# Pinning the cast and split of the re-read tokens to their place in the source

## The chip, the cores and the metric

The kernel runs on one core of one Trainium2 chip. The metric is the device time of one execution in microseconds (us); the median of several executions is compared. Lower is better.

The core has engines that run side by side and each take their own instructions in order: TensorE (PE in the profile; its weight loads are PEld), VectorE (DVE), ScalarE (ACT), GpSimd (POOL) and SyncE (SP), which here only starts DMA transfers. An instruction that must wait for another engine or for a transfer holds up everything behind it on its own engine.

## The reference, cut to what matters

One step of a hybrid decoder layer with 256 prompt tokens and 8 samples of 8 tokens each: a mixer (a pooling branch and a state-space branch, "SSD", with 64 heads in 8 groups), a cross-attention and a gated MLP. The change sits in the state-space branch, where the recurrent state of the 8 samples is brought up to date:

```python
def step(h, inp):
    s, d = inp
    return h * d[..., None, None] + s, h
...
chunk_states = jnp.einsum('bcsgn,bcsgr,bcsgrp->bcgrpn', bm, to_end, xd)
```

For every group and sample, the new state is the old one times a decay, plus a product over the sample's 8 tokens of their B row (128 numbers) and their weighted x row (512 numbers).

## The kernel before

All dense products work in three matmuls on fp32r operands: a weight tile of 128x1024 ("unit", `raw`) is loaded, cast to `wh` on ScalarE (L82), and its remainder `wl` is taken on VectorE (L83); then TensorE runs L88 (wh by the high part of the activations), L89 (wh by the low part) and L90 (wl by the high part). The buffers of `raw` are 4 deep, those of `wh` and `wl` 3, the accumulators `acc` 4 and the other PSUM tiles `misc` 4. One matmul of 320 columns follows the last after 0.15 us.

`mixer_ssd` goes through 8 groups. In each it writes out a list of dense jobs, and after a job the small steps of the state-space branch that `ssd` lists by job number. From the second to the seventh group the jobs are: 0 to 5 the six xBC columns of the next group, 6 to 13 the eight jobs `ssm_out` of the group before (24 matmuls each; their two sums are added into `accs` by VectorE at L711, in the second group copied by ScalarE at L709), then four gate jobs. In the first group jobs 6 to 9 are `gate_pool` columns of 48 matmuls, in the last one jobs 0 to 5 are.

The steps that matter here, with the job after which they are written:

- 4: `states`, whose result `fin` is stored, and `off_sample`
- 5: `diagonal` (matmuls L594, VectorE's sum L596 out of PSUM), and `rows_in(0)`, `rows_in(1)`: the sample tokens that were stored to DRAM are read again, each sample's 8 rows four times, into `rw` (two tiles of 128x640, L558)
- 6: `off_prompt` (matmuls L605, VectorE L606) and `off_sample_out` for both halves (transposes L201 into `misc`, VectorE L628); after job 7, `add_off` (GpSimd, L655)
- 8 and 10: `rows_split(0)`, `rows_split(1)`: ScalarE casts `rw` to `rh` (L565), VectorE takes from `rw` a part of `rh` that depends on the row (L568, once for 512 columns, once for 128)
- 9 and 12: `update(0)`, `update(1)`: four matmuls each (L644) on the split rows; VectorE adds them to the decayed state `hin` (L648)
- 9 and 11 of the next group's list: `decays` (VectorE L488, 24 small scalings of tables `g` and `gs_` that a DMA has brought, then exponentials on ScalarE, L490)

`rh`, `fin` and one more tile share one buffer (tag `fin`), so each cast L565 also waits until that buffer's last reader is done: the store of `fin`, or L568 of the half before. The xBC jobs end in three taps on VectorE (L443) between ScalarE's L441 and L447.

The program is not run in the order of writing. A scheduler reorders it at build time: it puts an instruction into its engine's queue when it believes its operands ready, by priority, and units are given a head start of 300 places. `keep_in_program_order(ins)` adds an edge for the order alone, without a wait: `ins` stands behind the instruction of its engine that was written last before it.

Of the kernel before, what the change touches and what calls it, by code (L numbers as in the profile page):

```python
# [11 lines left out]
F32 = mybir.dt.float32  # L12
F32R = mybir.dt.float32r
AF = mybir.ActivationFunctionType
ALU = mybir.AluOpType
# [42 lines left out]
class Kernel:  # L58
# [397 lines left out]
    def ssd(self, s, g):  # L456

        nc, I, O = self.nc, self.I, self.O
# [102 lines left out]
        def rows_split(q):  # L561

            rw = v["rw", q]
            rh = s.tile([128, 640], F32R, tag="fin", name="rh")
            nc.scalar.copy(out=rh, in_=rw)  # L565
            rr = v["rr"] = rw.bitcast(F32R)
            for c, w_ in ((C_RX, slice(0, 512)), (C_RB, slice(512, 640))):
                nc.vector.scalar_tensor_tensor(out=rr[:, w_], in0=rh[:, w_].bitcast(F32), scalar=self.cst[:, c:c + 1],  # L568
                                               in1=rw[:, w_], op0=ALU.mult, op1=ALU.add)

        def states():
            bt, xw = v["bt"], v["xw"]
# [81 lines left out]
        def add_off():  # L654
# [13 lines left out]
            6: [off_prompt, lambda: off_sample_out(0), lambda: off_sample_out(1)],  # L668
            7: [add_off],
            8: [lambda: rows_split(0)],  # L670
            9: [lambda: update(0)],
            10: [lambda: rows_split(1)],
            11: [lambda: store_states(0)],
            12: [lambda: update(1)],
# [595 lines left out]
```

## Time and profile before

| what | value |
|---|---|
| median of 3 executions | 2934.41 us (2933.08 to 2935.30) |
| profiled execution, its own time | 2932.04 us |
| its span | 2930.2 us |
| PE (matmul) busy | 2903.8 us, 99% |
| PEld busy | 2821.0 us, 96% |
| DVE busy | 1768.9 us, 60% |
| ACT busy | 1304.7 us, 45% |
| POOL busy | 454.4 us, 16% |
| granted TensorE clock, mean | 0.998 |

The profile shows one execution. Busy time is the time in which an engine had an instruction under way; matmul ends are modelled, so starts are the surer reading. A view by waits names the waiting instruction, the one that released it, the total in us, the number of times and the longest. A timeline row gives start and duration in us, engine, source line, operation, the tile written and those read, the shape, how many instructions are merged (x) and, in brackets, how long the engine had been idle before and who ended that.

### The profile page before, as it was taken

What the parts mean: (1) busy time and instruction counts of PE and PEld (TensorE: products, weight loads), DVE (VectorE), ACT (ScalarE), POOL (GpSimd) and SP (SyncE); (2) the same over time, 40 slices, a digit from 0 to 9 for tenths busy, and PEclk for the clock granted to TensorE, in tenths of its full rate; (3) what the DMA queues carried; (4) which work ended last, traced back from release to release, by engine and by line L of the source; (5) the groups of instructions that cost most, each with busy time, mean ns of one, the idle gap of its engine ahead of it and who ended that gap; (6) DMA issues with size and microseconds to landing.
All of it is one profiled execution on the core that took longest, in us unless ns stands there. A gap on an engine that the chain in (4) does not pass through costs nothing.

```text
span 2930.2 us, 50017 instructions
## 1 busy us (share of the span) xinstructions
PE 2903.8 (99%) x20105; PEld 2821.0 (96%) x20105; DVE 1768.9 (60%) x2662; ACT 1304.7 (45%) x1866; POOL 454.4 (16%) x567
## 2 busy tenths in 40 slices
PE   9999999999999999999999999999999999999998
PEld 7999999999999999999999999999999999999997
DVE  5667576686776755554355555567666646645644
ACT  6535565455454444344333443345444434433434
POOL 3113132142231220231111100011000000000002
PEclk9999999999999999999999999999999999999999
DMA  7775655655645645544445477754444444444443
GB/s 280 245 229 190 228 188 171 222 159 197 225 154 202 225 151 186 181 154 164 152 171 187 151 252 281 262 184 154 151 154 149 155 151 151 151 153 148 153 151 115
DMA packets 173385, 536.93 MB, mean 183 GB/s; under 512 B 21344, under 2 KB 48224, under 8 KB 168928
## 3 DMA queue, kind: packets, MB, share of 16 engines
q1 hardware_dynamic: 162272, 515.14, 52.1%
q10 hardware_dynamic: 10880, 18.58, 1.8%
q8 instruction: 158, 2.59, 0.4%
q14 instruction: 75, 0.61, 0.1%
HBM read 497.09 MB, written 36.56 MB: 182 GB/s over the span
## 4 chain that ended last, share of the span: by engine, by line
PE 84%; DVE 8%; issue 2%; ACT 2%; DMA 2%; POOL 2%; SPq 0%; POOLq 0%; ACTq 0%; DVEq 0%
PE acc L88 27%; PE acc L89 26%; PE acc L90 26%; DVE wl L83 3%; DVE ca L443 1%; POOL hin L637 1%; ACT wh L82 1%; DVE g L488 1%; DMA raw<-in_w_ssm_out_dram 1%; DVE accs L711 1%; PE misc L981 1%; PE misc L943 1%; PE acc L239 0%; PE acc L240 0%; PE acc L238 0%
## 5 line engine op out<-in xcount | busy, mean ns | idle before, releaser
L83 DVE TENSOR_TENSOR wl<-raw,wh 128x1024 fp32r<-128x1024 f32 (+1 forms) x795 | 986.9, 1242 | 808.7 <-ACT wh L82 807.1
L82 ACT CAST wh<-raw 128x1024 fp32r<-128x1024 f32 (+1 forms) x795 | 829.9, 1045 | 1207.1 <-PE acc L89 830.4
L88 PE MATMUL acc<-a0h,wh 128*128 128x320 f32 (+1 forms) x2704 | 837.2, 310 | 0.0
L90 PE MATMUL acc<-a0h,wl 128*128 128x320 f32 (+1 forms) x2704 | 831.7, 308 | 1.3 <-DVE wl L83 1.3
L89 PE MATMUL acc<-a0l,wh 128*128 128x320 f32 (+1 forms) x2704 | 831.6, 308 | 0.0
L88 PE MATMUL acc<-a1h,wh 128*128 128x320 f32 x1920 | 592.1, 308 | 0.1
L89 PE MATMUL acc<-a1l,wh 128*128 128x320 f32 x1920 | 590.7, 308 | 0.0
L90 PE MATMUL acc<-a1h,wl 128*128 128x320 f32 x1920 | 590.5, 308 | 0.0
L88 PEld LDWEIGHTS acc<-a0h,wh 128*128 128x128 f32 (+1 forms) x2704 | 505.9, 187 | 3.5 <-ACT wh L82 1.6
L89 PEld LDWEIGHTS acc<-a0l,wh 128*128 128x128 f32 (+1 forms) x2704 | 505.9, 187 | 2.2 <-issue 1.9
L90 PEld LDWEIGHTS acc<-a0h,wl 128*128 128x128 f32 (+1 forms) x2704 | 505.9, 187 | 1.9 <-DVE wl L83 1.7
L88 PEld LDWEIGHTS acc<-a1h,wh 128*128 128x128 f32 x1920 | 359.8, 187 | 3.8 <-issue 2.8
L89 PEld LDWEIGHTS acc<-a1l,wh 128*128 128x128 f32 x1920 | 359.8, 187 | 1.8 <-issue 1.7
L90 PEld LDWEIGHTS acc<-a1h,wl 128*128 128x128 f32 x1920 | 359.8, 187 | 0.0
L154 POOL TENSOR_TENSOR ssum<-ssum,sq 128x320 f32<-128x320 f32 x63 | 64.6, 1025 | 893.3 <-ACT sq L153 892.8
L88 PE MATMUL acc<-yh,wh 128*128 128x320 f32 x512 | 161.3, 315 | 3.5 <-DVE accs L711 3.2
L89 PE MATMUL acc<-yl,wh 128*128 128x320 f32 x512 | 158.0, 309 | 0.0
L90 PE MATMUL acc<-yh,wl 128*128 128x320 f32 x512 | 157.9, 308 | 0.0
L443 DVE SCALAR_TENSOR_TENSOR ca<-ext,vecs,ca 128x344 f32<-128x344 f32 x144 | 108.0, 753 | 6.0 <-ACT ca L441 4.1
L88 PEld LDWEIGHTS acc<-yh,wh 128*128 128x128 f32 x512 | 96.0, 187 | 9.0 <-issue 8.0
L1075 DVE SCALAR_TENSOR_TENSOR fca<-fext,vecs,fca 128x336 f32<-128x336 f32 x176 | 99.5, 566 | 3.1
L1070 POOL COPY fnew<-fext 128x18 f32<-128x18 f32 x88 | 18.5, 210 | 528.3 <-DVE fext L1069 528.3
(295 smaller groups left out, 3679.8 us busy)
## 6 DMA issues: line engine op xcount, KB each, us to landing
raw<-in_w_up_dram SPq DMA_DIRECT2D x176, 512.0 KB
raw<-in_w_xbc_dram SPq DMA_DIRECT2D x96, 512.0 KB
raw<-in_w_down_dram SPq DMA_DIRECT2D x88, 512.0 KB
raw<-in_w_z_dram SPq DMA_DIRECT2D x64, 512.0 KB
raw<-in_w_ssm_out_dram SPq DMA_DIRECT2D x64, 512.0 KB
raw<-in_w_mem_k_dram SPq DMA_DIRECT2D x32, 512.0 KB
hin<-in_state_ssm_dram SPq DMA_DIRECT2D x32, 512.0 KB
raw<-in_w_gp_dram SPq DMA_DIRECT2D x32, 512.0 KB
```

The source lines that it names most:

```text
L82: nc.scalar.copy(out=wh[:, c], in_=raw[:, c])
L83: nc.vector.tensor_tensor(out=wl[:, c], in0=raw[:, c], in1=wh[:, c].bitcast(F32), op=ALU.subtract)
L88: nc.tensor.matmul(out, lhsT=wh, rhs=xh, start=first, stop=False)
L89: nc.tensor.matmul(out, lhsT=wh, rhs=xl, start=False, stop=False)
L90: nc.tensor.matmul(out, lhsT=wl, rhs=xh, start=False, stop=last)
L154: nc.gpsimd.tensor_tensor(out=ssum, in0=ssum, in1=sq, op=ALU.add)
L443: nc.vector.scalar_tensor_tensor(out=ca[:, 0:344], in0=e[:, j:j + 344], scalar=self.vec(V_CW + 48 * j + c), in1=ca[:, 0:344], op0=ALU.mult ...
L488: nc.vector.tensor_scalar(out=e[:n, h], in0=e[:n, h], scalar1=self.t_la[:n, j, h0 + h:h0 + h + 1], scalar2=0.0, op0=ALU.subtract, op1=ALU.min)
L637: nc.gpsimd.tensor_tensor(out=t.rearrange("p b (h d) -> p b h d", h=8), in0=t.rearrange("p b (h d) -> p b h d", h=8), in1=bcast(self.dec[: ...
L711: nc.vector.tensor_tensor(out=dst, in0=dst, in1=a, op=ALU.add)
L943: nc.tensor.matmul(ps[32 * b:32 * b + 32, :MEM], lhsT=qs[h % 2][:, dc, 4 * q + b], rhs=v["k", q][:, dc // 2, b, dc % 2], start=dc == 0, st ...
L1075: nc.vector.scalar_tensor_tensor(out=ca[:, :336], in0=e[:, j:j + 336], scalar=self.vec(V_FW + 88 * j + c), in1=ca[:, :336], op0=ALU.mult, ...
```

## The change

The three instructions of `rows_split` are pinned: the cast on ScalarE and the two splits on VectorE are each put behind the instruction of their engine that the source has last before them. For the splits that is, from the third group on, the second addition L711 of job 8 (for `rows_split(0)`) or job 10 (for `rows_split(1)`). For the casts it is most often a weight cast that the scheduler has moved far ahead anyway. What is computed stays the same.

```diff
             rh = s.tile([128, 640], F32R, tag="fin", name="rh")
-            nc.scalar.copy(out=rh, in_=rw)
+            self.tc.keep_in_program_order(nc.scalar.copy(out=rh, in_=rw))
             rr = v["rr"] = rw.bitcast(F32R)
             for c, w_ in ((C_RX, slice(0, 512)), (C_RB, slice(512, 640))):
-                nc.vector.scalar_tensor_tensor(out=rr[:, w_], in0=rh[:, w_].bitcast(F32), scalar=self.cst[:, c:c + 1],
-                                               in1=rw[:, w_], op0=ALU.mult, op1=ALU.add)
+                self.tc.keep_in_program_order(nc.vector.scalar_tensor_tensor(
+                    out=rr[:, w_], in0=rh[:, w_].bitcast(F32), scalar=self.cst[:, c:c + 1],
+                    in1=rw[:, w_], op0=ALU.mult, op1=ALU.add))
```

Lines behind L568 stand one line lower in the changed kernel (L596 becomes L597, L644 L645, L711 L712). On VectorE in the fourth group, from the weight split behind `fin` on, the queue was:

```order
L83 TENSOR_TENSOR wl<-raw,wh 128x1024
L568 SCALAR_TENSOR_TENSOR rw<-rh,cst,rw 128x512
L568 SCALAR_TENSOR_TENSOR rw<-rh,cst,rw 128x128
L596 SCALAR_TENSOR_TENSOR y<-x,vecs,misc 128x320
L83 TENSOR_TENSOR wl<-raw,wh 128x1024
L443 SCALAR_TENSOR_TENSOR ca<-ext_2131,vecs,ca 128x344
L596 SCALAR_TENSOR_TENSOR y<-x,vecs,misc 128x320
```

The splits of the first half stood ahead of the diagonal's sums L596, and those of the second half (not printed) between the two additions of job 6. In the changed kernel the same stretch reads:

```order
L83 TENSOR_TENSOR wl<-raw,wh 128x1024
L597 SCALAR_TENSOR_TENSOR y<-x,vecs,misc 128x320
L83 TENSOR_TENSOR wl<-raw,wh 128x1024
L597 SCALAR_TENSOR_TENSOR y<-x,vecs,misc 128x320
L443 SCALAR_TENSOR_TENSOR ca<-ext_2131,vecs,ca 128x344
L597 SCALAR_TENSOR_TENSOR y<-x,vecs,misc 128x320
```

and the splits of the first half now stand behind the additions of job 8, with a weight split between them, and just ahead of the additions of job 9:

```order
L712 TENSOR_TENSOR accs<-accs,acc 128x320
L568 SCALAR_TENSOR_TENSOR rw<-rh,cst,rw 128x512
L83 TENSOR_TENSOR wl<-raw,wh 128x1024
L568 SCALAR_TENSOR_TENSOR rw<-rh,cst,rw 128x128
L712 TENSOR_TENSOR accs<-accs,acc 128x320
L488 TENSOR_SCALAR gs__2136<-gs__2136,t_la 64x64 x4
```

So L596 (now L597) lost two predecessors, and the splits moved some 20 places down, to a place where the update's matmuls are the next users. TensorE's own queue is the same from the second group on.

In the first group, VectorE's queue ahead of the first additions to the state (L649) becomes:

```order
L488 TENSOR_SCALAR gs__2136<-gs__2136,t_la 64x64 x4
L83 TENSOR_TENSOR wl<-raw,wh 128x1024 x3
L568 SCALAR_TENSOR_TENSOR rw<-rh,cst,rw 128x512
L568 SCALAR_TENSOR_TENSOR rw<-rh,cst,rw 128x128
L649 TENSOR_TENSOR hin<-hin,misc 128x512
```

There the splits now stand behind three weight splits, of which the last belongs to the second unit of job 8; TensorE's update matmuls stand four matmuls into job 8 instead of ahead of it. On ScalarE in that group the cast L565, which stood with the first weight casts after the store of `fin`, now comes behind a `gate_pool` result and one more weight cast:

```order
L719 ACTIVATE gp<-acc 128x320
L82 CAST wh<-raw 128x1024
L720 DMA gp_dram<-gp 128x320
L565 CAST rh<-rw 128x640
L82 CAST wh<-raw 128x1024
```

From the fourth group on, the first cast L565 moved behind one weight cast and the two copies L436 and L437, and the second one behind two exponentials.

## Rows read from the trace of the kernel before

**Rows 1.** Waits of PE, whole run: waiting, released by, us in total, times, longest.

```profile
PE misc L201 <- DVE y L596: 5.4, 12, 0.9
PE acc L88 <- DVE accs L711: 3.2, 5, 0.9
```

**Rows 2.** Timeline of PE, fourth group (start us, us, instruction, count, idle before).

```profile
637.21 0.66 PE L201 MATMUL misc<-cst,ye 128*128 128x128 f32 x4 [0.67 <-DVE y L596]
638.16 0.66 PE L201 MATMUL misc<-cst,ye 128*128 128x128 f32 x4 [0.29 <-DVE y L596]
...
649.30 0.50 PE L644 MATMUL misc<-rw 32*128 32x512 f32 x4
...
656.73 0.31 PE L90 MATMUL acc<-yh,wl 128*128 128x320 f32 x1
657.67 0.39 PE L88 MATMUL acc<-yh,wh 128*128 128x320 f32 x1 [0.64 <-DVE accs L711]
...
661.37 0.50 PE L644 MATMUL misc<-rw 32*128 32x512 f32 x4
```

**Rows 3.** Timeline of DVE, fourth group.

```profile
631.26 1.23 DVE L83 TENSOR_TENSOR wl<-raw,wh 128x1024 fp32r<-128x1024 f32 x1 [1.54 <-ACT wh L82]
633.60 1.02 DVE L568 SCALAR_TENSOR_TENSOR rw<-rh,cst,rw 128x512 fp32r<-128x512 f32 x2 [1.11 <-ACT rh L565]
634.53 0.54 DVE L596 SCALAR_TENSOR_TENSOR y<-x,vecs,misc 128x320 f32<-128x320 f32 x1
...
638.02 0.57 DVE L443 SCALAR_TENSOR_TENSOR ca<-ext,vecs,ca 128x344 f32<-128x344 f32 x1
...
638.97 0.48 DVE L711 TENSOR_TENSOR accs<-accs,acc 128x320 f32<-128x320 f32 x1
...
640.69 1.22 DVE L83 TENSOR_TENSOR wl<-raw,wh 128x1024 fp32r<-128x1024 f32 x1
641.82 0.68 DVE L606 TENSOR_TENSOR yo<-misc,el 128x512 f32<-128x512 f32 x1
642.42 0.47 DVE L628 TENSOR_TENSOR yo<-misc,el 128x128 f32<-128x128 f32 x2
642.82 2.08 DVE L488 TENSOR_SCALAR g<-g,t_la 128x128 f32<-128x128 f32 x2
...
645.22 1.25 DVE L488 TENSOR_SCALAR g<-g,t_la 128x128 f32<-128x128 f32 x6
...
650.30 0.56 DVE L488 TENSOR_SCALAR gs__2136<-gs__2136,t_la 64x64 f32<-64x64 f32 x3
```

**Rows 4.** Timeline of ACT, fourth group.

```profile
632.84 0.73 ACT L565 CAST rh<-rw 128x640 fp32r<-128x640 f32 x1 [1.61 <-DMA out_ssm_prompt_dram<-fin]
...
638.66 0.51 ACT L447 ACTIVATE x<-ca,vecs 128x256 f32<-128x256 f32 x1
639.07 0.33 ACT L448 ACTIVATE x<-ca,vecs 128x64 f32<-128x64 f32 x1
639.31 1.04 ACT L82 CAST wh<-raw 128x1024 fp32r<-128x1024 f32 x1
```

**Rows 5.** Timeline of POOL, fourth group.

```profile
642.98 1.84 POOL L655 TENSOR_TENSOR y<-y,yo 128x768 f32<-128x768 f32 x1 [3.97 <-DVE yo L628]
```

**Rows 6.** Timeline of DVE, first group.

```profile
297.63 1.07 DVE L488 TENSOR_SCALAR g<-g,t_la 128x128 f32<-128x128 f32 x5 [0.45 <-DMA g<-la_dram]
...
312.73 1.23 DVE L83 TENSOR_TENSOR wl<-raw,wh 128x1024 fp32r<-128x1024 f32 x1 [1.46 <-ACT wh L82]
```

**Rows 7.** Timeline of ACT, first group.

```profile
303.06 1.06 ACT L490 ACTIVATE g<-g 128x1024 f32<-128x1024 f32 x1 [4.32 <-DVE g L488]
...
311.65 1.04 ACT L82 CAST wh<-raw 128x1024 fp32r<-128x1024 f32 x1
```

**Rows 8.** Timeline of PE, first group.

```profile
306.98 0.41 PE L90 MATMUL acc<-a0h,wl 128*128 128x320 f32 x1 [1.30 <-DVE wl L83]
...
310.40 0.51 PE L644 MATMUL misc<-rw 32*128 32x512 f32 x4
```

## The prediction

> **What bounds the kernel now.** I read the share of busy time first: PE is busy nearly the whole span, so only time in which PE stands still can be won. Next the waits of PE over the whole run [rows 1]. Two entries touch the place of the change: transposes of `off_sample_out` wait for the diagonal's sums L596 on DVE (5.4 us, 12 times: two in each of six groups), and `ssm_out` matmuls wait for the additions L711 (3.2 us, 5 times). Together 8.6 us, 0.3% of the run: that is all the change can win there, apart from one wait in the first group [rows 8]. Then the timelines of one group. I take the fourth, whose waits are near the mean: PE idles 0.67 and 0.29 us before the transposes (mean of six groups 5.4 / 6 = 0.90) and 0.64 us before a later `ssm_out` job (3.2 / 5 = 0.64) [rows 1, 2].
>
> Why PE waits there is on DVE [rows 3]: at 633.60 stand the two splits L568, after 1.11 us of idling for the cast L565, and only then comes the first L596. The transposes need PSUM tiles that L596 must empty. The cast came late since it waited for the store of `fin` out of its own buffer [rows 4]. From 633.60 on DVE shows no more such wait: it runs behind PE, and late additions hold the accumulators that job 12 wants at 657.67.
>
> **What the change does, with prices.** Nothing is added or removed but order edges; 16 casts and 32 splits move. A pair of splits takes 0.93 us of DVE (633.60 to 634.53), a weight split L83 1.13 us (640.69 to 641.82) [rows 3].
>
> First, the diagonal. L596 follows the L83 of 631.26 directly: 631.26 + 1.13 = 632.39 instead of 634.53, 2.1 us earlier, and the other sums follow likewise. Their weight cast on ACT no longer stands behind L565. So both waits for L596 go: PE reaches the first update L644 0.96 us earlier, at 649.30 - 0.96 = 648.34 [rows 2].
>
> Second, the update. L644 never waits for DVE today, since the splits were done 10 us before. Now DVE must first get to them. From 634.53 to 650.30 it does 15.77 us of work [rows 3], of which the second pair of splits (0.93) goes: 14.84, so it is through at 632.39 + 14.84 = 647.23. One table scaling has moved ahead of that point: 0.56 / 3, some 0.2 us [rows 3]. And one new wait shows up. DVE gets to the L83 of 640.69 sooner: the work from 634.53 to 642.42 is 7.89, less 0.93 and less that L83, 5.83, so 632.39 + 5.83 = 638.22. Its cast on ACT stands behind L447 and L448, which follow the last tap L443. The last tap's place now ends 4.44 us after the first L596 (634.53 to 638.97 [rows 3]), at 636.83, its write 0.08 later (0.57 in a place of 0.49); L447 starts 0.07 after that, as before (638.02 + 0.57 against 638.66), the cast 0.65 later and takes 1.04 [rows 3, 4]: 638.67. DVE waits 0.5 us. Sum: 647.23 + 0.2 + 0.5 = 647.9. Then the pair with an L83 in its middle, 1.02 + 1.13 = 2.15 [rows 3]: 650.1. L644 starts at 650.1, 0.8 us later than before, and PE has waited 650.1 - 648.3 = 1.8 us for it: a new wait in place of the old ones.
>
> Third, the accumulators. From L644 to the last matmul before the wait at 657.67 PE takes 656.73 + 0.15 - 649.30 = 7.58 us [rows 2]. From 650.1 that gives 657.68. By then DVE has only 1.1 us of splits behind it that it did not have to do before, and the additions of job 10 come some 1.5 us earlier than today, so the wait of 0.64 is gone. PE is at 657.7, as before, and at the second update at 661.4, as before. The second pair of splits stands behind the additions of job 10 and is done some 3 us ahead of its update. **The group comes out even, 0.0 us**: three waits go, one comes. The third, fifth, sixth and seventh group have the same queues and the same waits to some tenths; I take them at 0.0 too. Bounds for each of these five: -1.6 us (all three waits go, none comes), +1.0 us (first rival).
>
> In the second group ACT empties the accumulators and DVE waits for a table; the 0.9 us before the transposes go, and the pair of splits (1.0) comes in ahead of the update. I take 0, with bounds -0.9 and +1.0. In the eighth PE has no wait for L596 and DVE is not late: 0.
>
> **The first group** costs. Its splits now stand behind the weight split of 312.73, which waits 1.46 us for its cast on ACT, and the cast stands in an unbroken row of ACT work that starts with the exponential of 303.06, held by DVE's scalings [rows 6, 7]. Those wait for a table (0.45 us at 297.63 [rows 6]). The table's load is started when the second L83 of the diagonal frees a weight buffer, and that moves forward by the first pair of splits, 0.9 us, and some idling: 1.0 us. So the cast comes at 310.65, the L83 at 311.73 and ends its place at 312.87, the pair at 312.87 + 1.02 = 313.9. L644 stood at 310.40 and now stands four matmuls later (4 x 0.15 = 0.6) [rows 8]: 313.9 - 310.40 - 0.6 = **2.9 us** lost. PE itself would have been there at 310.0, since the wait of 1.30 us at 306.98 shrinks by the same 1.0. No wait later in that group takes it back. Bounds: -1.3 (that wait goes, no new one) and +3.9.
>
> Sum: 5 x 0.0 + 0 + 2.9 = +2.9 us. On the profiled execution 2932.04 + 2.9 = 2934.9; the median of the runs shown is 2.37 above it, 2934.41 + 2.9 = **2937.3 us**. PE work, loads and clock are the same otherwise; what measurement can tell from no change is about 0.2%, 5.9 us.
>
> **A rule weighed against a row.** The vector work of 15.77 us has 1.6 us in it in which DVE did nothing useful: two scalings took 2.08 us at 642.82, where six take 1.25 at 645.22 [rows 3], while GpSimd's addition L655 ran from 642.98 for 1.84 us [rows 5]. That addition starts right behind L628, so my sum keeps the collision. The Trainium skill, "SBUF — State Buffer", section "Who interferes with whom", says that VectorE and GpSimd share one pair of ports as an exclusive lock, and that issue order decides who blocks. The trace agrees that the later one stood still for the whole addition (0.2 us of work took 1.8). By that rule, a vector queue that has moved may meet the addition from the other side and not be blocked; that is the second rival.
>
> **Rivals.**
> Slower: the decay tables do not come earlier. Their loads could be held by the traffic, not by the freed buffer. DVE would then wait at the scalings until 642.82, where it could be at 638.70 + 1.13 + 0.40 = 640.23 [rows 3]; of these 2.59 us the collision of 1.6 is spent meanwhile, so L644 comes 1.0 us later still, in five groups. 2937.3 + 5.0 = 2942.3. For it: in the first group the table is what DVE waits for [rows 6]. Against: in the fourth it had landed when DVE came. It decides from about 0.5 us of waiting. Chance 0.17.
>
> Faster: the update does not wait, since DVE is 1.6 us sooner (the collision falls away) and the 0.5 us for the cast too. Then each of the five groups wins 0.96 + 0.64 = 1.6 us, 8.0 in all: 2929.3; with the second group and the start-up of the matmuls behind each wait 2928. For it: GpSimd's addition waits for DVE, so it can shift. Against: DVE is busy when it starts, whatever is next in line. Chance 0.12.
>
> No net change at all: the first group's cast is ready in time, or its loss is hidden, and the rest is even: 2934.4. For it: ACT's order there leaves it two table loads that could fall better. Against: the queue as built puts the splits behind that weight split. Chance 0.16.
>
> **How the numbers follow.** My forecast has 0.53, the three rivals 0.45, 0.02 is left for anything else. Faster by over 0.2% takes most of the faster rival, 0.09; slower by over 0.2% takes the slower rival but its low end, and the tail of the forecast (0.4 us more in each of five groups and a little in the first), 0.19; 0.72 is left for the same. The range reaches to both rivals' times without their far ends: 2929.5 to 2942.5.
>
> **What would show it.** Right: PE's waits for L596 and L711 are gone or under 1 us, and a wait of the update matmuls for L568 on DVE stands in their place, 1.5 to 2 us in each of five groups and 3 to 4 us in the first, 11 to 14 us in all; in the fourth group the first update starts 18.8 us after the L83 behind `fin` (18.0 before), the second 30.1 (30.1 before). Wrong: no such wait, or well under 1 us (then faster), or over 2.5 us (then slower); scalings on DVE that wait for the table; a first group whose updates start no later.

## The result, and the profile after

The changed kernel takes 2956.68 us (median of 4 runs, 2951.99 to 2959.54), the kernel before 2934.14 us on the same chip. The ratio is 1.0079, with a 95% interval of 1.0067 to 1.0091: slower by 0.8%, some 22 us. Forecast were 2937.3 us and a range up to 2942.5. The prediction was wrong.

The profiled execution is the fastest of the four, 2951.99 us with a span of 2950.2, so what follows explains 20.0 us (2950.2 - 2930.2). The other three have a mean granted clock of 0.993 to 0.994, where the profiled one has 0.995 and the kernel before 0.998; where they lose more no trace shows.

The waits of PE over the whole run, the answer to [rows 1] (waiting, released by, us in total, times, longest; "issue": no releaser was found):

```profile
PE misc L645 <- issue: 19.7, 7, 3.5
PE acc L90 <- DVE wl L83: 1.9, 2, 1.3
```

The 5.4 us before the transposes and the 3.2 us before `ssm_out` are gone, as forecast. In their place the first update waits in seven of eight groups, 19.7 us in all. Against the 8.6 us that are gone, that is 11.1 us more standing still. The rest is in the first line of the page: PE itself is busy 2911.8 us, where it was 2903.8, with the same 20105 matmuls.

```profile
PE 2911.8 (99%) x20105; PEld 2832.1 (96%) x20105; DVE 1762.4 (60%) x2662; ACT 1304.3 (44%) x1866; POOL 447.7 (15%) x567
```

So the kernel loses some 11 us by waiting and 8.0 us by slower matmuls. Since ends of matmuls are modelled, this split is rough; by starts, further down, the part behind the waits is the larger one. The fourth group shows both. PE's timeline (start us, us, instruction, count, idle before), the answer to [rows 2]:

```profile
658.97 0.30 PE L90 MATMUL acc<-yh,wl 128*128 128x320 f32 x1
662.15 0.84 PE L645 MATMUL misc<-rw 32*128 32x512 f32 x4 [2.88 <-issue]
...
663.47 0.30 PE L88 MATMUL acc<-yh,wh 128*128 128x320 f32 x1
663.61 0.32 PE L89 MATMUL acc<-yl,wh 128*128 128x320 f32 x1
...
663.99 0.47 PE L88 MATMUL acc<-yh,wh 128*128 128x320 f32 x1
664.26 0.47 PE L89 MATMUL acc<-yl,wh 128*128 128x320 f32 x1
...
667.35 0.31 PE L89 MATMUL acc<-yl,wh 128*128 128x320 f32 x1
...
675.22 0.50 PE L645 MATMUL misc<-rw 32*128 32x512 f32 x4
```

The update waits 2.88 us. Its matmuls start at 662.15, and the dense ones behind them follow at first 0.15 us from start to start, as usual; from 663.8 on, 1.6 us after the wait ended, they follow 0.27 us from start to start, until about 667. The same stretch by 2 us (us, busy time and count of PE, PEld, DVE, ACT, POOL, granted clock, DMA share, GB/s):

```profile
658.00:660.00 2.00, 1.27 (x9) 1.01 (x7) 2.00 (x9) 0.53 (x1) 0.00 (x0) 1.00 0.45 124
660.00:662.00 2.00, 0.00 (x0) 0.00 (x0) 2.00 (x4) 0.53 (x1) 0.00 (x0) 1.00 0.41 166
662.00:664.00 2.00, 1.85 (x11) 1.63 (x12) 2.00 (x8) 1.68 (x2) 0.00 (x0) 0.95 0.57 164
664.00:666.00 2.00, 2.00 (x9) 2.00 (x9) 2.00 (x4) 0.00 (x0) 0.00 (x0) 0.50 0.30 107
666.00:668.00 2.00, 2.00 (x12) 2.00 (x11) 1.42 (x3) 0.00 (x0) 0.00 (x0) 0.70 0.86 188
668.00:670.00 2.00, 2.00 (x16) 2.00 (x15) 1.71 (x3) 1.05 (x1) 0.00 (x0) 1.00 0.99 406
```

The granted clock falls to 0.50, that is from 2.4 to 1.2 GHz, here behind the wait and not in it, with PE at work again. In the seventh group the update waits 2.19 us (at 1009.36), and the clock stays at 1.00:

```profile
1009.00:1011.00 2.00, 1.64 (x10) 1.42 (x11) 2.00 (x8) 1.66 (x2) 0.00 (x0) 1.00 0.39 98
1011.00:1013.00 2.00, 2.00 (x15) 2.00 (x15) 2.00 (x4) 0.02 (x1) 0.00 (x0) 1.00 0.41 164
```

VectorE in the fourth group, the answer to [rows 3]:

```profile
642.56 1.23 DVE L83 TENSOR_TENSOR wl<-raw,wh 128x1024 fp32r<-128x1024 f32 x1 [1.54 <-ACT wh L82]
643.71 0.54 DVE L597 SCALAR_TENSOR_TENSOR y<-x,vecs,misc 128x320 f32<-128x320 f32 x1
...
651.12 0.48 DVE L629 TENSOR_TENSOR yo<-misc,el 128x128 f32<-128x128 f32 x2
653.82 0.68 DVE L488 TENSOR_SCALAR g<-g,t_la 128x128 f32<-128x128 f32 x3 [2.22 <-DMA g<-la_dram]
...
659.52 0.47 DVE L712 TENSOR_TENSOR accs<-accs,acc 128x320 f32<-128x320 f32 x1
659.92 0.73 DVE L568 SCALAR_TENSOR_TENSOR rw<-rh,cst,rw 128x512 fp32r<-128x512 f32 x1
660.58 1.21 DVE L83 TENSOR_TENSOR wl<-raw,wh 128x1024 fp32r<-128x1024 f32 x1
661.72 0.33 DVE L568 SCALAR_TENSOR_TENSOR rw<-rh,cst,rw 128x128 fp32r<-128x128 f32 x1
```

PE finished job 9 at 659 and wants the split rows; VectorE starts them at 659.92, behind an addition of job 8, and is through at 662.0. The first sum L597 follows its weight split at once, as forecast.

By group, from the timelines of both kernels: the time from the weight split behind `fin` to the first update, and from the first update to the second, in us.

| group | to the first update, before / after | first to second update, before / after |
|---|---|---|
| 1 | 25.88 / 30.69 | 21.95 / 23.15 |
| 2 | 18.44 / 19.49 | 11.19 / 13.08 |
| 3 | 17.98 / 19.88 | 12.38 / 13.05 |
| 4 | 18.04 / 19.59 | 12.07 / 13.07 |
| 5 | 17.88 / 19.43 | 12.23 / 13.05 |
| 6 | 18.32 / 19.96 | 12.07 / 13.06 |
| 7 | 18.34 / 19.30 | 11.63 / 11.53 |
| 8 | 18.05 / 17.77 | 11.18 / 11.20 |

The differences add up to 19.7 us of the 20.0; outside these stretches next to nothing changed.

### The profile page after: what moved, and what is told of

It reads as the page before. It is cut to its first block, busy times and chain, and to the rows that moved or that the text cites. A ratio compares the mean times of both kernels' runs of the same rounds, so it can differ in the third digit from the quotient of the medians.

```text
span 2950.2 us, 50032 instructions
## 1 busy us (share of the span) xinstructions
PE 2911.8 (99%) x20105; PEld 2832.1 (96%) x20105; DVE 1762.4 (60%) x2662; ACT 1304.3 (44%) x1866; POOL 447.7 (15%) x567
## 4 chain that ended last, share of the span: by engine, by line
PE 95%; issue 1%; DMA 1%; ACT 1%; POOL 1%; DVE 1%; SPq 0%; ACTq 0%; POOLq 0%
PE acc L88 30%; PE acc L89 30%; PE acc L90 29%; PE misc L201 1%; PE misc L595 1%; PE misc L982 1%; PE misc L944 1%; PE misc L618 1%; ACT wh L82 0%; POOL sx L154 0%; PE misc L645 0%; DMA g<-la_dram 0%; DVE wl L83 0%; PE acc L239 0%; PE misc L577 0%
```

## The experiments

Each ran on one chip together with runs of the kernel before, whose median is given. Theory A was made from the traces of both kernels: the update waits for the splits that are pinned one job ahead of it, and a low clock follows.

**Which of the pins.** Only the splits on VectorE pinned:

```diff
-            self.tc.keep_in_program_order(nc.scalar.copy(out=rh, in_=rw))
+            nc.scalar.copy(out=rh, in_=rw)
```

> Only the two splits on VectorE are pinned, the cast on ScalarE is free. Theory A (the loss comes from the update's matmuls waiting for the pinned splits, and from the low TensorE clock behind each such wait): the second to the seventh group keep their loss (2.9 + 4 x 2.5 + 0.9 = 13.8 us by the traces), while in the first group, where the free cast lets the splits stand ahead of the table scalings, the loss of 6.0 goes: about 2956.7 - 6.0 = 2950.7 us. Theory B (the cast, moved behind other ScalarE work, makes the splits late): about 2934 us, no waits for L568.

2949.91 us against 2931.73, ratio 1.0060 [1.0045, 1.0075]. Only the cast pinned, the splits as before:

```diff
-            nc.scalar.copy(out=rh, in_=rw)
+            self.tc.keep_in_program_order(nc.scalar.copy(out=rh, in_=rw))
```

> Only the cast on ScalarE is pinned, the splits on VectorE are free. By the queue as built the sums L596 then go first and the splits of the first half stand between the additions of job 6, some 10 us ahead of the update; in the first group they stand behind three weight splits as in the whole change. Theory A: no update wait from the third group on, the waits for L596 gone (-0.96 us x 5), the loss of 6.0 us in the first group kept: 2934.1 + 6.0 - 4.8 = 2935 us (2930 to 2939). Theory B: as slow as the whole change, 2956 us.

2935.28 us, ratio 1.0012 [1.0002, 1.0021]. Both times came as theory A said, but the two pins share the loss by groups. From the weight split behind `fin` to the second update, the run with the splits alone loses 2.1 to 4.5 us in each of the third to the seventh group and nothing in the first two (-2.0 and -0.3 us); the run with the cast alone loses 5.6 and 3.9 us in the first two and nothing behind them. So the pins on VectorE carry the loss of the later groups, the pin of the cast that of the first two. The second run held a surprise. Its waits of PE from 515 us on, that is from the third group:

```profile
PE acc L88 <- DVE accs L711: 3.2, 4, 1.0
```

No wait for L596, none at an update. With the cast held back behind the copies L436 and L437, the sums go first and the splits stand where nobody waits, between the additions of job 6. In the fourth group the first update comes 16.65 us after the weight split, where it came after 18.04. In this run the third to the eighth group win 7.3 us by their timelines, and the first two lose 9.5. In the second, the update waits:

```profile
432.29 0.90 PE L644 MATMUL misc<-rw 32*128 32x512 f32 x4 [2.94 <-issue]
```

**Which group.** All pinned, but not in the first group (`if g`):

> All three instructions pinned, but not in the first group. Theory A: the first group's 6.0 us go, the rest stays: 2956.7 - 6.0 = 2950.7 us, with the waits of the later groups unchanged. A rival by which the late first group drags the later ones along (their tables and weights come late because of it): 2934 to 2940 us.

2949.97 us, ratio 1.0061 [1.0044, 1.0078]: the first group is worth 4 to 5 us, and the later groups lose on their own.

**Which half.** Pinned in the second half only (`if q == 1`):

> Pinned in the second half only (rows_split(1)); the first half's cast and splits are free, and stand ahead of the sums L596 as in the kernel before. Theory A (the loss is the first half's update, which comes only one job behind its pinned splits): no loss; the waits for L596 stay, those for L711 (0.64 us in five groups) go: 2931.7 - 3.2 = 2928.5 us (2926 to 2932). Rival E (the second half's splits, three matmul jobs ahead of their update, are late too): 2936 us or more, with waits at the second update.

2930.49 us against 2932.80, ratio 0.9992 [0.9983, 1.0001]. Two waits of its list:

```profile
PE misc L201 <- DVE y L598: 5.0, 12, 0.8
...
PE acc L88 <- DVE accs L713: 0.9, 2, 0.7
```

The second half's pins do no harm: the waits for the additions shrink from 3.2 to 0.9 us, and no update waits.

**The place of the pin.** The first half's cast and splits written after job 6:

```diff
-            6: [off_prompt, lambda: off_sample_out(0), lambda: off_sample_out(1)],
+            6: [off_prompt, lambda: off_sample_out(0), lambda: off_sample_out(1), lambda: rows_split(0)],
...
-            8: [lambda: rows_split(0)],
```

> All pinned, but the cast and split of the first half are written after job 6, not job 8: on VectorE they then stand behind the sums L596 and L629 and ahead of the table scalings, where the whole change has VectorE idle for the table (1.90 us in one group). Theory A: no update wait, no low clock, the waits for L596 and L711 gone: 2934.1 - 5 x 1.6 = 2926 us (2923 to 2930). Rival C (VectorE is short of time in these jobs wherever the splits stand, so another wait comes up instead): 2934 us or more.

2929.11 us against 2931.73, ratio 0.9990 [0.9981, 1.0000]. The update does not wait, but the old waits are not gone as expected: 4.5 us for the sums and 2.2 for the additions stay. On ScalarE the first half's cast still stands ahead of a weight cast and waits for the store of `fin`; in the fourth group the weight split behind it waits 1.84 us, and the sums with it:

```profile
632.63 0.73 ACT L565 CAST rh<-rw 128x640 fp32r<-128x640 f32 x1 [1.85 <-DMA out_ssm_prompt_dram<-fin]
```

The first update one job later:

```diff
-            9: [lambda: update(0)],
-            10: [lambda: rows_split(1)],
-            11: [lambda: store_states(0)],
+            10: [lambda: update(0)],
+            11: [lambda: rows_split(1), lambda: store_states(0)],
```

> All pinned where the change has them, but the first update is written one job later (after job 10 instead of 9; rows_split(1) after it). Theory A: PE comes to the update 24 matmuls (3.5 us) later and finds the splits done, so no wait over 0.5 us and no low clock from the third group on; the waits for L596 and L711 stay gone; in the first group 48 matmuls hide the 3.25 us, and 2.2 us of waits for a weight split stay: 2931.7 - 5 x 1.6 + 2 = 2926 us (2923 to 2931). Rival F (with the splits so late VectorE falls behind, and the additions to the state hold the PSUM tiles or the accumulators of later jobs): 2934 us or more.

2942.53 us against 2932.80, ratio 1.0035 [1.0022, 1.0049]: a miss. Both updates of the fourth group:

```profile
654.67 0.51 PE L645 MATMUL misc<-rw 32*128 32x512 f32 x4
...
665.36 0.63 PE L645 MATMUL misc<-rw 32*128 32x512 f32 x4 [2.96 <-DVE rw L568]
```

The first update no longer waits; the second does, since my edit had moved its own splits to one job ahead of it. The wait goes with the distance between pin and use, not with the half. With both updates one job later and the splits where the change has them:

```diff
-            9: [lambda: update(0)],
-            10: [lambda: rows_split(1)],
+            10: [lambda: update(0), lambda: rows_split(1)],
...
-            12: [lambda: update(1)],
+            13: [lambda: update(1)],
...
-                             enumerate([(1,), (2,), (), (4,), (5,), (6,), (7, 8), (9,), (10,), (11,), (12,), (14,)])}
+                             enumerate([(1,), (2,), (), (4,), (5,), (6,), (7, 8), (9,), (10,), (11,), (12, 13), (14,)])}
```

The last two lines give the first group's shorter list its step 13.

> The whole change, with both updates one job later (after jobs 10 and 13) and the splits where the change pins them (after 8 and 10). In the run in which only the first update was later and the second half's splits were pinned one job later with it, the first update waited no more and the second waited 3 us in its place. Theory A (a pinned split needs more than one job, 24 matmuls, ahead of its update): no update wait from the second group on, the waits for L596 and L711 gone, some 2 us lost in the first group: 2932 - 8 + 2 = 2926 us (2923 to 2930). Rival F (VectorE is behind whatever the place): 2936 us or more.

2931.03 us against 2933.13, ratio 0.9991 [0.9982, 1.0000]. The largest wait of its list:

```profile
PE acc L88 <- DVE accs L711: 8.1, 9, 1.5
```

No update waits. But of the 7 us hoped for, 2 came: VectorE is late with the accumulators, presumably since splits and additions to the state now stand close together. Rival F had that mechanism, with too high a price.

**The tables.** The largest hole in VectorE's row is the wait of 2.22 us for `g`. Was that why it came late to the splits?

```diff
+        self.g_ = [s.tile([128, 8, 128], F32, name=f"g{j}") for j in range(2)] + [self.gs_]
...
-                e = s.tile([128, 1024], F32, tag="g", name="g", bufs=2).rearrange("p (h t) -> p h t", h=8) if j < 2 else self.gs_
+                e = self.g_[j]
...
-                nc.sync.dma_start(out=e[:n], in_=bcast(src, [n, 8, n]))
+                if g < 2:
+                    nc.sync.dma_start(out=e[:n], in_=bcast(src, [n, 8, n]))
```

> The whole change, but from the third group on the decay tables g and gs_ are not loaded again: the buffers of the second group are used on, so the state-space branch computes with wrong decays (left out: 1.2 MB of loads per group). What VectorE and TensorE have to do is the same. Theory A (VectorE comes late to the pinned splits since it waits for the tables): without that wait of 1.9 us the update waits about 1 us in place of 2.9 in the third to the seventh group, and no low clock follows: on this kernel before of some 2932 us, where the whole change gives 2955, 2955 - 5 x (1.9 + 1.7) = 2937 us (2934 to 2944). Rival H (the splits are late because of the additions and weight splits they stand behind, and the wait for the tables is spare time): 2950 us or more, update waits near 3 us.

2950.35 us against 2933.13, ratio 1.0058 [1.0044, 1.0071]: the time is rival H's. The timelines of DVE, POOL and PE in the fifth group:

```profile
764.96 2.28 DVE L490 TENSOR_SCALAR g<-g,t_la 128x128 f32<-128x128 f32 x3
...
769.33 1.21 DVE L490 TENSOR_SCALAR gs__2136<-gs__2136,t_la 64x64 f32<-64x64 f32 x7
```
```profile
765.12 1.84 POOL L658 TENSOR_TENSOR y<-y,yo 128x768 f32<-128x768 f32 x1 [3.64 <-DVE yo L631]
```
```profile
774.80 0.84 PE L647 MATMUL misc<-rw 32*128 32x512 f32 x4 [2.84 <-issue]
```

VectorE does not wait for a table any more, but then GpSimd's addition catches three scalings, which take 2.28 us, where three took 0.68 while VectorE had sat out the addition waiting for the table. So 1.6 us of the table's wait (1.90 us in the fifth group of the change) come back as the collision. The update stands 19.55 us behind the weight split, in the change itself 19.43. But the edit did more than take out the wait: without the loads seven more scalings of `gs_` (1.21 us) go ahead of the splits, eight where the change has one. Without them, by an estimate from these rows, the splits would have come about 1 us sooner. So the run shows that most of the wait is not what makes the splits late; it does not show that the wait costs nothing.

**The clock.** To measure what follows a wait, 1 to 6 copies of the split rows onto themselves were put on VectorE ahead of each update of the second to the seventh group, in the kernel with the split after job 6:

```diff
             rr = v["rr"]
+            keep = self.tc.keep_in_program_order
+            for _ in range(({1: 1, 2: 3, 3: 5, 4: 2, 5: 4, 6: 6}, {1: 2, 2: 4, 3: 6, 4: 3, 5: 1, 6: 5})[q].get(g, 0)):
+                keep(nc.vector.tensor_copy(out=rr[:, :512], in_=rr[:, :512].bitcast(F32)))
```

The update's matmuls, and the first one behind them, were pinned as well.

> The kernel with the first half's splits after job 6, with 1 to 6 copies of the split rows onto themselves on VectorE put ahead of each update of the second to the seventh group (copies ahead of first/second update: 1/2, 3/4, 5/6, 2/3, 4/1, 6/5), and the update's matmuls held in place. What is computed stays the same. It gives PE waits of known and growing length, some 0.5 us per copy. Theory A (a wait of about 2.3 us and more is followed by matmuls at half clock, which cost 1.8 us more): after waits under 2 us the granted clock stays 1.00 and the way to the next landmark is as before; after those of 3 us it falls to 0.50 for some 3 us. Rival D (the slow stretch in the changed kernel has another cause): the clock stays 1.00 behind all of them.

The copies cost more than expected, 2994.37 us in a single run, with waits of 0.9 to 7.8 us. Two of them, in rows of 2 us; ahead of 812.00 PE had waited 2.85 us, ahead of 687.07 it had waited 4.23:

```profile
810.00:812.00 2.00, 0.00 (x0) 0.00 (x0) 1.91 (x4) 0.14 (x1) 0.00 (x0) 1.00 0.19 74
812.00:814.00 2.00, 2.00 (x14) 1.76 (x15) 1.46 (x3) 0.00 (x0) 0.00 (x0) 1.00 0.68 215
814.00:816.00 2.00, 2.00 (x16) 2.00 (x15) 1.41 (x3) 0.00 (x0) 0.00 (x0) 1.00 0.75 303
```
```profile
685.00:687.00 2.00, 0.00 (x0) 0.00 (x0) 1.90 (x5) 0.00 (x0) 0.00 (x0) 1.00 0.30 84
687.00:689.00 2.00, 1.94 (x10) 1.69 (x11) 1.41 (x4) 0.00 (x0) 0.00 (x0) 0.65 0.45 178
689.00:691.00 2.00, 2.00 (x9) 2.00 (x9) 1.08 (x2) 0.00 (x0) 0.00 (x0) 0.50 0.62 250
691.00:693.00 2.00, 2.00 (x16) 2.00 (x15) 0.63 (x2) 0.28 (x1) 0.00 (x0) 1.00 0.97 318
```

The low clock follows long waits, whatever makes them; rival D falls. But "3 us" as the point from which it does is not what the runs show. Over this run, the change and the five others in which updates waited, 42 waits of the update of over 0.9 us in all, measured between starts of matmuls (from the start of the last one to the start of the one that waited, less the usual step of 0.15): the two under 2.3 us (1.08 and 2.16) were followed by no fall, of 24 between 2.3 and 3.2 us 19 were, and all 16 longer ones. Each fall cost 1.1 to 2.3 us in the dense matmuls behind the update, also behind waits of 7 us. In the middle it goes both ways: the change itself has one of 2.33 us with a fall and one of 2.34 without.

Nor does it take a wait of the update. In three runs (the split after job 6, the copies put on top of it, both updates later) the clock also fell in the first group, behind a wait for a weight split of 1.9, 1.9 and 1.31 us of idle time. The last, in the run with both updates later:

```profile
307.42 0.42 PE L90 MATMUL acc<-a0h,wl 128*128 128x320 f32 x1 [1.31 <-DVE wl L83]
```
```profile
306.00:308.00 2.00, 0.69 (x4) 0.58 (x4) 1.36 (x3) 1.97 (x4) 1.43 (x1) 0.95 0.00 0
308.00:310.00 2.00, 2.00 (x10) 2.00 (x9) 0.00 (x0) 1.99 (x3) 0.00 (x0) 0.50 0.77 240
```

In the kernel before the same wait was 1.30 us [rows 8], and the clock stayed at 1.00. In each of the three runs the fall costs some 1.5 us that the expectation did not have.

**A version that is faster than both.** The cast alone pinned, from the third group on:

```diff
-            nc.scalar.copy(out=rh, in_=rw)
+            ins = nc.scalar.copy(out=rh, in_=rw)
+            if g > 1:
+                self.tc.keep_in_program_order(ins)
```

> Only the cast is pinned, and only from the third group on; the splits are free. In the run with the cast pinned everywhere the third to the eighth group were shorter by 1.45, 0.85, 1.67, 1.63, 1.42 and 0.28 us from the weight split behind fin to the second update, the first two longer by 5.6 and 3.9. Theory A: the gain stays and the loss goes: 2931.7 - 7.3 = 2924.4 us (2922 to 2928). Rival G (the later groups were short only because the first two had come late and their loads early): 2931 to 2933 us.

2924.11 us against 2932.80, ratio 0.9969 [0.9958, 0.9981], as theory A had it. What is left of the waits at this place:

```profile
PE acc L88 <- DVE accs L713: 2.3, 4, 0.9
...
PE misc L201 <- DVE y L598: 1.1, 2, 0.8
```

With the second half's splits pinned too:

> From the third group on: both casts pinned, and the splits of the second half; the splits of the first half are free. In the run with the casts alone four groups kept a wait of 0.5 to 1.2 us for the additions L711, ahead of which the second half's free splits stand. Theory A: that wait goes, 4 x 0.8: 2924 - 3 = 2921 us (2919 to 2924). Rival E (the second half's splits come late to their update then): 2926 us or more.

2923.61 us against 2933.13, ratio 0.9968 [0.9957, 0.9980]: no better than the cast alone. The waits for the additions fell from 2.3 to 1.2 us, and those of other matmuls for a weight split (L239) rose from 0.2 to 1.4 us.

## Why the prediction was wrong

**The mechanism was right.** The waits for the sums and the accumulators go, and a wait of the first update for L568 stands in their place, with the chain of work that the prediction went through. It gave 18.8 us from the weight split to the first update in the fourth group and 30.1 to the second; the trace has 19.59 and 32.66.

**The step that failed is the third, "the accumulators", with the sentence "PE work, loads and clock are the same otherwise".** It let PE go on from L644 "to the last matmul before the wait" in the 7.58 us of before, and wrote "PE is at 657.7, as before". That holds only if a wait costs PE nothing but its length. From the first to the second update, less the wait for the accumulators, the kernel before took 12.07 - 0.80 = 11.27 us in the fourth group (the 0.80 between starts: 657.67 - 656.73 less the usual 0.15 [rows 2], rounded); the changed one takes 13.07. These 1.8 us had no term in the sum, no bound and no rival of their own; the start-up of the matmuls behind a wait is named, but only in the faster rival's sum. By the table such extra time is 1.8 us in the first group (1.2, and 0.6 for the four matmuls that now stand ahead of the update), 1.9 in the second, 1.8 in each of the third to the sixth and 0.3 in the seventh: 11.2 of the 19.7 us. Some 0.3 us of each is the update's own matmuls starting anew (0.84 us for four where they took 0.50), the rest the half clock. With that term alone the forecast would have been 2937.3 + 11.2 = 2948.5 us.

The rows of before gave no sign of the clock: no wait in [rows 1] or [rows 8] is over 1.30 us, and none is followed by a fall. But the sum itself had waits of 1.8 and 3 to 4 us in it that no row of before shows. The Trainium skill, "TensorE: Matmul & The Clock Gate", section "HAM oscillation — how this bites in real kernels", tells of a kernel whose idle gaps between bursts of matmuls bring the half clock back, gaps longer than most of the waits here. The trace agrees that a wait can bring it back (0.50 in 664 to 666, behind one of 2.88 us), and the runs above show it behind shorter ones; the prediction weighed none of this.

**The size of the new wait** was the second error: 19.7 - 11.2 = 8.5 us are left for it, where the forecast had 2.9 in all. Point by point:

- *Third to seventh group, even.* The update came 1.9, 1.55, 1.55, 1.64 and 0.96 us later than before, forecast 0.8 each. In the fourth group the pair starts 17.36 us after the weight split (659.92 - 642.56), forecast 647.9 - 631.26 = 16.64. What comes back later, the accumulators' waits, is 4.0 us between starts, as forecast to some tenths. Without what follows the waits these groups lose some 3.6 us, not 0.
- *The tables.* The sum let them come sooner with the freed buffer. In the fourth group their loads do start sooner, 3.5 us behind the weight split where it had been 5.4, but VectorE gets to the scalings at 651.6 and waits until 653.82, 11.26 us behind the weight split, where the scalings had begun at 11.56 [rows 3]. That was the slower rival's condition, a table held by something other than the buffer. Its price came in part: the wait is 2.22 us, and as it said the collision of 1.6 "is spent meanwhile", so 0.6 us are left of the 1.0 that it asked for. The pair comes 0.7 us later than forecast (17.36 - 16.64).
- *First group.* Forecast +2.9, bound +3.9, measured 4.8 to the first update, of which 0.6 is its later place: 4.2, just past the bound. The table's load does start 1.1 us sooner (287.81 after, 288.94 before), as the step with "that moves forward" said. But VectorE can go on with the table no sooner (297.65 after, 297.63 before), the last weight split starts at 312.74 where it had 312.73, and PE's wait of 1.30 us for a weight split is not shorter. The step took the start of a load for its landing.

```profile
297.65 1.07 DVE L488 TENSOR_SCALAR g<-g,t_la 128x128 f32<-128x128 f32 x5 [0.38 <-DMA g<-la_dram]
...
312.74 1.22 DVE L83 TENSOR_TENSOR wl<-raw,wh 128x1024 fp32r<-128x1024 f32 x1 [1.46 <-ACT wh L82]
313.89 1.01 DVE L568 SCALAR_TENSOR_TENSOR rw<-rh,cst,rw 128x512 fp32r<-128x512 f32 x2
```

- *Second group, 0 with +1.0 as bound.* It is at the bound, 1.05 us, and has a low clock behind it.
- *The faster rival.* GpSimd's addition did shift, as it supposed: in the changed kernel VectorE sits it out while it waits for the table. It won nothing, since the wait for the table is the longer of the two.
- *What would show it.* The waits of the update, "11 to 14 us in all" by the prediction, came out at 19.7; "over 2.5 us (then slower)" was met.

Without what follows the waits the time would have been 2934.1 + 8.5 = 2942.6 us, just at the end of the range. Some 2 us of the 11.2 are the new starts (7 x 0.3), some 9 the half clock. So the clock is the largest single term that was missing, but not the only one that took the time past the range.

## What to carry to other kernels

An order edge moves an instruction to its place in the source; what counts is how far that place is from the next user, and how late the engine runs there. Here 24 matmuls (3.5 us) between pin and use were too few: in the fourth group the addition that the splits were pinned behind ran at 659.52, 4.1 us after TensorE had started its job's last matmul. The pin on the cast alone, from the third group on, left the splits to the scheduler and won 8.7 us, where the whole change loses 22. Where an edit makes TensorE wait in a place where it never waited, price the wait and also the matmuls behind it, and do so before taking old waits off against the new one.

## What the runs showed of the hardware that was not expected

- Behind most waits of the update TensorE first ran at full clock (1.6 us in the fourth group) and then at 1.2 GHz for some 3 us, in the midst of uninterrupted matmuls: 0.27 us from start to start in place of 0.15. Behind the longest waits (6 to 8 us between starts), and behind three of 3.0, 3.1 and 3.7 us, the clock was low from the update on.
- No length of wait that decides can be read from these runs: 2.33 us with a fall, and 3.16 us without one, both occurred; and for a weight split in the first group 1.31 us with a fall and 1.30 without.
- The wait for a table and the collision with GpSimd's addition are not added up: 2.22 us of the one or 1.6 us (2.28 - 0.68) of the other. Where VectorE waited out a part of the addition, its next scaling lost only the rest (in the seventh group of the change a wait of 1.21 us, then a scaling of 0.80).
